# A two-layer trunk on one core: mask order in the DeltaNet layer, and wide products for most output blocks and the value blocks of three batches

## The chip, the cores and the metric

The kernel runs on one core of a Trainium2 chip. The metric is the device time of one execution in microseconds (us); lower is better. The kernel before takes 2536.62 us (median of three runs, 2536.11 to 2537.5).

## The reference

Input x has 256 tokens of 2048 channels, in float32. Two layers follow each other. Layer 0 is differential attention and a gated feed-forward block with a short causal convolution; layer 1 is a gated DeltaNet and a second feed-forward block. Each of the four parts is normalised ahead and added to x behind. The change lies in the DeltaNet, whose reference is, cut:

```python
def gated_deltanet(h, w_in, conv_w, a_log, dt_bias, norm_g, w_out):
    proj = h @ w_in
    qkv, z, b_gate, a_gate = jnp.split(proj, [...], axis=-1)
    qkv = jax.nn.silu(causal_dwconv(qkv, conv_w))
    q, k, v = jnp.split(qkv, [GDN_KEY_DIM, 2 * GDN_KEY_DIM], axis=-1)
    q = l2_norm(q...); k = l2_norm(k...)
    ...
    o = gated_delta_rule(q, k, v, g, beta)
    o = rms_norm(o, norm_g) * jax.nn.silu(z...)
    return o.reshape(...) @ w_out
```

There are 16 heads of queries and keys and 32 of values, each 128 wide. Inside the delta rule a decay `exp(g_i - g_j)` is taken where i >= j and zero elsewhere, and for every chunk of 64 tokens a triangular system is solved.

## The kernel before, in words

Activations lie transposed in SBUF: channels on the 128 partitions, tokens along the free axis. For precision every float32 operand is split into a rounded part and the rest: a weight tile becomes `whi` (ScalarE, line 89) and `wlo` (VectorE, line 90), and an activation has its two parts side by side. A product of a weight tile with an activation tile is three terms: high by high, low by high, high by low.

`dense` (line 132) makes one block: 128 or 256 output channels for 256 tokens, over 16 input tiles (8 in an output block of the DeltaNet), loaded four at a time from HBM into one of four slots. It has two forms. Wide: one product of 512 columns takes `whi` against both parts of the activation, and writes the two results beside each other in PSUM, and one of 256 columns takes `wlo` against the first part (lines 151 and 152). Narrow: three products of 256 columns, all added in the same 256 columns of PSUM (lines 151, 152 and 154). A pair of PSUM tiles (`ps`, two buffers) takes blocks by turns.

How a block leaves PSUM depends on the form. `merge` (line 177) multiplies a narrow block by the norm factor in one VectorE operation (line 196). A wide block has its second half copied by ScalarE (line 199), added by VectorE (line 200) and scaled by VectorE (line 205). `add_x` (line 340) adds a narrow block to x with one VectorE operation and a wide one with two (line 343). The feed-forward blocks are wide; in the DeltaNet all `dense` blocks are narrow.

The DeltaNet (`gdn`, line 542) does its 16 heads in four batches of four. The plan of a batch is: four blocks of queries and keys (k), the first block of values (v), two gate blocks (z, by `dense_tok`), and the other three blocks of values. Then come the eight output blocks of the batch before; those of the last batch follow at the end. Behind the blocks, generators go on one step at each `tick`, which `dense` calls after every load of four tiles: `keys` (per head: normalisation, decay, products of keys), `invert` (per batch: a triangular inversion in steps on VectorE, lines 654 and 657, with transposes in lines 661 and 663), `levels` (small products that finish the inverse, lines 691 to 725), `to_tokens` and `group` (the outputs of a pair of heads, lines 739 to 803, which leave the tiles `oc` for the output blocks).

What sets the order is this order of writing together with a planner, which simulates the time of every instruction when the kernel is built and so lays out each engine's list. On the chip each engine works off its list in order.

In `keys` a head squares its queries and keys (line 589), splits the squares in two parts (lines 321 and 322, tile `qp`, one buffer), fetches its decay rows from HBM by a broadcast DMA (line 594, tile `lt`), which can only begin once the gates' rows have been written there (line 902), adds the mask to them (line 610), sums the squares over the partitions on TensorE (`total`, line 329), takes an inverse root and the exponentials on ScalarE (lines 613 to 616) and scales (line 617). Two steps later the products of keys follow (lines 624 and 625).

Of the kernel before, what the change touches and what calls it, by code (L numbers as in the profile page):

```python
# [8 lines left out]
F32 = mybir.dt.float32  # L9
F32R = mybir.dt.float32r  # L10
AF = mybir.ActivationFunctionType
ALU = mybir.AluOpType
# [7 lines left out]
KD = D // P  # L20
# [6 lines left out]
class Trunk:  # L27
# [37 lines left out]
    def mp(self):  # L65
        return self.mps.tile([P, 512], F32, tag="mp", name="mp")
# [252 lines left out]
    def split(self, out, a):  # L319

        self.nc.scalar.copy(out[:, 0], a)
        self.nc.vector.tensor_tensor(out[:, 1], a, out[:, 0].bitcast(F32), ALU.subtract)

    def total(self, out, parts):

# [216 lines left out]
    def gdn(self, w_gate, w_in, w_z, w_out, nb, hb, gate_ap, const_ap, conv_col, ng, done):  # L542
# [7 lines left out]
        nc, tc, mp = self.nc, self.tc, self.mp  # L550
        nq = nb * hb
# [3 lines left out]
        with tc.tile_pool(name="gd", bufs=1) as gd:  # L555
# [13 lines left out]
                nc.gpsimd.memset(Tas[i][:64], 0.0)  # L569
            quad = [slice(32 * s, 32 * s + 32) for s in range(4)]  # L570
            flat = "p i c -> p (i c)"
            gates = {}

            def lin(ps):
                u = gd.tile([P, 2, T], F32, tag="u", name="u", bufs=1)
                self.merge(ps, u)
                return u

            def convs(u, tiles):
                c = gd.tile([P, 2, T], F32, tag="cv", name="cv", bufs=4)  # L580
                for i in range(2):
                    self.conv(c[:, i, :], u[:, i, :], [conv_col(t, tiles[i]) for t in range(4)], None)
                nc.scalar.activation(c, c, AF.Silu)
                return c

            def keys(hq, c, cc, b0, res):

                sq = gd.tile([P, 2, T], F32, tag="qs", name="qs", bufs=2)
                nc.scalar.square(sq, c)
                sp = gd.tile([P, 2, 2, T], F32R, tag="qp", name="qp", bufs=1)  # L590
                self.split(sp, sq)
                def fetch():
                    d = gd.tile([P, 2, 384], F32, tag="lt", name="lt", bufs=hb)
                    nc.sync.dma_start(d, gates["rows"][2 * hq:2 * hq + 2, :].unsqueeze(0).to_broadcast([P, 2, 384]))
                    return d

                d = fetch() if "rows" in gates else None
                yield
                yield
                while "rows" not in gates:  # L600
                    yield
                if d is None:
                    d = fetch()
                    yield
                    yield
                    yield
                gc = gates["col"]
                dv = d[:, :, :T].rearrange("p v (t c) -> p v t c", t=2)
                m4 = mask.unsqueeze(1).unsqueeze(1).to_broadcast([P, 2, 2, P])
                nc.vector.tensor_tensor(dv, dv, m4, ALU.add)  # L610
                pn = mp()
                with self.lnexp(self.total(pn, [sp])):
                    self.rsqrt(sq, self.apart(pn), 1)
                    for v in range(2):
                        for t, s in ((1, d[:, v, :P]), (0, d[:, v, P:])):
                            nc.scalar.activation(s, s, AF.Exp, bias=gc[:, t, 2 * hq + v:2 * hq + v + 1])
                nc.vector.tensor_tensor(c, c, sq, ALU.mult)
                q, k = c[:, 0, :], c[:, 1, :]
                yield
                yield  # L620
                prods = []
                for r in (k, q):
                    p = mp()
                    nc.tensor.matmul(p[:, :P], k[:, P:], r[:, P:], start=True, stop=True)
                    nc.tensor.matmul(p[:, P:384], k[:, :P], r, start=True, stop=True)  # L625
                    prods.append(p)
                lt = d
                qkt = gd.tile([P, 2, 384], F32, tag="qkt", name="qkt", bufs=hb)
                for v in range(2):
                    nc.vector.scalar_tensor_tensor(  # L630
                        qkt[:, v], prods[1][:, :384], P ** -0.5, d[:, v], ALU.mult, ALU.mult)
                    nc.vector.tensor_tensor(lt[:, v], prods[0][:, :384], d[:, v], ALU.mult)
                for v in range(2):
                    b = b0 + v
                    lv = lt[:, v, :T].rearrange("p (t c) -> p t c", t=2)
                    for r in quad:
                        nc.gpsimd.tensor_copy(
                            cc[r, :, 2 * b:2 * b + 2].rearrange("p c t -> p t c"), lv[r, :, r])
                    res.append((lt[:, v], qkt[:, v]))
# [89 lines left out]
            def to_tokens(c, vt, g, ready):  # L729
                yield  # L730
                yield
                p = mp()
                for t in range(2):
                    for i in range(2):
                        nc.tensor.transpose(p[:, (2 * t + i) * P:(2 * t + i + 1) * P], c[:, i, t * P:(t + 1) * P], ident)  # L735
                nc.scalar.copy(vt[:, :, g:g + 2, :], p.rearrange("p (t v c) -> p t v c", t=2, v=2))
                ready.append(g)
# [66 lines left out]

            def out(b, acts):
                for blk in range(KD // 2):
                    ps = self.dense(w_out[b * (KD // 2) + blk], 2 * hb, lambda k: self.await_(acts, k), wide=False)
                    self.add_out(blk, ps, done if b == nb - 1 else None, False)

            pg = self.dense(w_gate, KD, self.h_acts, tiles=1, wide=False)  # L810
            self.spawn(self.gates(gd, pg, nv, gp, ident, early, gates))
# [1 line left out]
            for b in range(nb):  # L813
                heads = range(b * hb, (b + 1) * hb)
                cc = gd.tile([P, 32, 32], F32, tag="s4", name="Cc", bufs=3)
                nc.gpsimd.memset(cc, 0.0)
                lqs, inv, solved, acts, zts = [], [], [], [], {}
                groups = [range(i, i + gh) for i in range(0, hb, gh)]
                plan = [("k", i) for i in range(hb)] + [("v", 0)] + [("z", g) for g in range(len(groups))]
                for op, i in plan + [("v", i) for i in range(1, hb)]:  # L820
                    if op == "k":
                        hq = heads[i]
                        c = convs(lin(self.dense(w_in[hq * 2], KD, self.h_acts, wide=False)), (hq, nq + hq))
                        self.spawn(keys(hq, c, cc, 2 * i, lqs))
                        if i == hb - 1:
                            self.spawn(invert(cc, lqs, inv))
                            self.spawn(levels(lqs, inv, range(len(groups)), solved))
                    elif op == "z":
                        gr = groups[i]
                        zt = zts[i] = gd.tile([P, 2, gv, P], F32, tag="vz", name="zt", bufs=4)  # L830
                        ps = self.dense_tok(w_z[heads[gr[0]] // 2], KD, self.h_acts)
                        for t in range(2):
                            nc.scalar.activation(zt[:, t].rearrange(flat), ps[:, t, :], AF.Silu,
                                                 scale=self.rstdc[:, t:t + 1])
                    else:
                        gi = i // gh
                        gr = groups[gi]
                        if i == gr[0]:
                            vt = gd.tile([P, 2, gv, P], F32, tag="vz", name="vt", bufs=4)
                            ready = []  # L840
                            self.spawn(group(gi, gr, lqs, solved, vt, ready, zts, acts))
                        hq = heads[i]
                        c = convs(lin(self.dense(w_in[hq * 2 + 1], KD, self.h_acts, wide=False)),
                                  (2 * nq + 2 * hq, 2 * nq + 2 * hq + 1))
                        self.spawn(to_tokens(c, vt, 2 * (i - gr[0]), ready))
                if pend:
                    out(*pend)
                pend = (b, acts)
            out(*pend)

    def gates(self, gd, pg, nv, gp, ident, early, res):
# [210 lines left out]
```

## Time and profile before

| | |
|---|---|
| Median of three runs | 2536.62 us |
| The profiled execution, whole | 2537.79 us |
| Its span, first to last instruction | 2536.1 us |
| The DeltaNet, from its first gate product to the last output product | 1054.5 to 1855.5 us |
| Granted TensorE clock | 1.000 |

In the rows that follow, PE is TensorE's products and PEld its weight loads, DVE is VectorE, ACT is ScalarE, SPq is the queue that issues the weights' DMAs. Lines such as L151 are lines of the kernel. A row of the timeline gives start, duration, engine, line, operation, output and inputs, and in brackets the idle time of that engine ahead of it with what released it. A group's row gives count, total busy time, mean duration in ns, and idle time before.

### The profile page before, as it was taken

To read this page: it belongs to the slowest core of one execution; us is meant where nothing else is said; L and a number is where in the kernel's file an instruction comes from. 1 tells how busy PE (TensorE), PEld (TensorE's weight loads), DVE (VectorE), ACT (ScalarE), POOL (GpSimd) and SP (SyncE) were. 2 spreads that over 40 slices of the span, in tenths; PEclk is the share of its full clock that TensorE was granted. 3 is DMA by queue.
4 is the path that set the end of the run, shared out by engine and by line. 5 is a ranking of instruction groups with operands and counts; after the bars stand their busy time and mean duration, and the time that the engine had idled before them with its cause. 6 is when DMAs were issued, how large, how long until landed. Compare 5 with 4: busy or idle time off the path is not lost.

```text
span 2536.1 us, 44059 instructions
## 1 busy us (share of the span) xinstructions
PE 2527.5 (100%) x17431; PEld 2354.5 (93%) x17431; DVE 1898.8 (75%) x2790; ACT 1505.4 (59%) x2076; POOL 91.6 (4%) x189
## 2 busy tenths in 40 slices
PE   9999999999999999999999999999999999999999
PEld 8998899999999999999999999999999999999998
DVE  8886677777777555679878788788787777776544
ACT  7766656666666444485674674674566666665443
POOL 0000000000000000010111011021000000000000
PEclk9999999999999999999999999999999999999999
DMA  7555566666666666666555565555466666666665
GB/s 254 176 183 174 167 205 201 201 201 201 201 202 202 198 203 201 201 192 199 161 174 184 167 185 179 171 182 178 159 200 201 202 200 202 201 201 207 208 208 157
DMA packets 138207, 487.34 MB, mean 192 GB/s; under 512 B 15472, under 2 KB 18448, under 8 KB 138000
## 3 DMA queue, kind: packets, MB, share of 16 engines
q1 hardware_dynamic: 137712, 484.17, 60.5%
q8 instruction: 137, 2.24, 0.4%
q14 instruction: 70, 0.57, 0.1%
q10 hardware_dynamic: 288, 0.35, 0.1%
HBM read 482.32 MB, written 2.15 MB: 191 GB/s over the span
## 4 chain that ended last, share of the span: by engine, by line
PE 99%; DMA 1%; DVE 0%; ACT 0%; SPq 0%; issue 0%
PE ps L151 47%; PE ps L152 27%; PE ps L154 7%; PE ps L220 3%; PE ps L221 3%; PE ps L222 3%; PE mp L752 2%; PE mp L151 1%; PE mp L329 1%; PE mp L625 1%; PE mp L152 0%; PE ps L123 0%; PE mp L717 0%; PE mp L735 0%; DMA raw<-w_first 0%; PE mp L797 0%
## 5 line engine op out<-in xcount | busy, mean ns | idle before, releaser
L90 DVE TENSOR_TENSOR wlo<-raw,whi 128x1024 fp32r<-128x1024 f32 (+2 forms) x911 | 1102.9, 1212 | 513.7 <-ACT whi L89 505.6
L89 ACT CAST whi<-raw 128x1024 fp32r<-128x1024 f32 (+2 forms) x911 | 944.4, 1038 | 864.7 <-PE ps L151 554.8
L151 PE MATMUL ps<-h,whi 128*128 128x512 f32 (+1 forms) x4208 | 1327.0, 356 | 0.0
L152 PE MATMUL ps<-h,wlo 128*128 128x256 f32 x4208 | 1151.0, 274 | 0.0
L151 PEld LDWEIGHTS ps<-h,whi 128*128 128x128 f32 x4208 | 798.3, 190 | 83.6
L152 PEld LDWEIGHTS ps<-h,wlo 128*128 128x128 f32 x4208 | 807.7, 192 | 0.9
L151 PE MATMUL ps<-ac,whi 128*128 128x512 f32 x1546 | 506.8, 382 | 0.0
L152 PE MATMUL ps<-ac,wlo 128*128 128x256 f32 x1546 | 421.2, 273 | 0.0
L151 PEld LDWEIGHTS ps<-ac,whi 128*128 128x128 f32 x1546 | 292.1, 189 | 40.8 <-PE ps L151 0.2
L152 PEld LDWEIGHTS ps<-ac,wlo 128*128 128x128 f32 x1546 | 296.8, 192 | 0.1
L154 PE MATMUL ps<-h,whi 128*128 128x256 f32 x1040 | 287.1, 276 | 0.0
L154 PEld LDWEIGHTS ps<-h,whi 128*128 128x128 f32 x1040 | 199.5, 192 | 0.4
L220 PE MATMUL ps<-whi,h 128*128 128x512 f32 x384 | 146.5, 382 | 0.0
L221 PE MATMUL ps<-wlo,h 128*128 128x512 f32 x384 | 146.0, 380 | 0.0
L222 PE MATMUL ps<-whi,h 128*128 128x512 f32 x384 | 145.9, 380 | 0.0
L310 DVE SCALAR_TENSOR_TENSOR cv<-u,fcols,cv 128x255 f32<-128x255 f32 (+1 forms) x344 | 142.7, 476 | 0.0
L151 PE MATMUL ps<-oc,whi 128*128 128x256 f32 x512 | 142.3, 278 | 0.0
L154 PE MATMUL ps<-oc,whi 128*128 128x256 f32 x512 | 141.9, 277 | 0.0
L152 PE MATMUL ps<-oc,wlo 128*128 128x256 f32 x512 | 141.5, 277 | 0.0
L154 PEld LDWEIGHTS ps<-oc,whi 128*128 128x128 f32 x512 | 98.2, 192 | 0.3
L152 PEld LDWEIGHTS ps<-oc,wlo 128*128 128x128 f32 x512 | 98.3, 192 | 0.2
L151 PEld LDWEIGHTS ps<-oc,whi 128*128 128x128 f32 x512 | 98.3, 192 | 0.1
(220 smaller groups left out, 2240.8 us busy)
## 6 DMA issues: line engine op xcount, KB each, us to landing
raw<-w_up SPq DMA_DIRECT2D x344, 512.0 KB, 4.8
raw<-w_down SPq DMA_DIRECT2D x160, 512.0 KB, 4.1
raw<-w_in SPq DMA_DIRECT2D x128, 512.0 KB, 4.6
raw<-w_z SPq DMA_DIRECT2D x64, 512.0 KB, 3.8
raw<-w_out SPq DMA_DIRECT2D x64, 512.0 KB, 4.3
raw<-w_qk SPq DMA_DIRECT2D x56, 512.0 KB, 4.6
raw<-w_v SPq DMA_DIRECT2D x32, 512.0 KB, 3.6
raw<-w_o SPq DMA_DIRECT2D x32, 512.0 KB, 4.5
```

The costliest lines, as they stand in the source:

```text
L89: self.cast = nc.scalar.copy(hi[:, :, s], raw[:, :, s])
L90: nc.vector.tensor_tensor(lo[:, :, s], raw[:, :, s], hi[:, :, s].bitcast(F32), ALU.subtract)
L151: nc.tensor.matmul(bank[c][:, :n], hi[:, k, s], self.turns(a[:, :n // T, :]), start=first, stop=False)
L152: nc.tensor.matmul(bank[c][:, :T], lo[:, k, s], self.turns(a[:, :1, :]), start=False, stop=last and wide)
L154: nc.tensor.matmul(bank[c][:, :T], hi[:, k, s], self.turns(a[:, 1:, :]), start=False, stop=last)
L220: nc.tensor.matmul(ps[:, c, :], ah, wh, start=first, stop=False)
L221: nc.tensor.matmul(ps[:, c, :], ah, wl, start=False, stop=False)
L222: nc.tensor.matmul(ps[:, c, :], al, wh, start=False, stop=last)
L310: nc.vector.scalar_tensor_tensor(out[:, j:], u[:, :T - j], taps[n - 1 - j], out[:, j:], ALU.mult, ALU.add)
L329: last = self.nc.tensor.matmul(out, self.onesr, self.pairs(p[:, j]), start=i + j == 0, stop=i + j == n)
L625: nc.tensor.matmul(p[:, P:384], k[:, :P], r, start=True, stop=True)
L752: nc.tensor.matmul(p[:, v, :], l(v), r[:, v, :], start=i == 0, stop=i == len(terms) - 1)
```

## The change

Three things are edited.

- Mask order. `split` returns its VectorE instruction, and `keys` keeps these in a list. The sum over partitions is written ahead of the mask addition. A head then goes on only when the first two heads have split their squares, and the mask addition is queued on VectorE behind a split: head 0's behind that of head 1, any other head's behind its own. Only head 0 waits for longer by this than before.
- Output blocks. All eight blocks of the last batch, and the last four of each of the other three batches, are wide.
- Value blocks. All four of each of the first three batches are wide. `lin` now calls `dense` itself, and for a wide block copies the second half into `u`, adds the first and scales, without a further tile.

```diff
     def split(self, out, a):
         self.nc.scalar.copy(out[:, 0], a)
-        self.nc.vector.tensor_tensor(out[:, 1], a, out[:, 0].bitcast(F32), ALU.subtract)
+        return self.nc.vector.tensor_tensor(out[:, 1], a, out[:, 0].bitcast(F32), ALU.subtract)
...
-            gates = {}
+            gates, lows = {}, []
-            def lin(ps):
+            def lin(w, wide):
+                ps = self.dense(w, KD, self.h_acts, wide=wide)
                 u = gd.tile([P, 2, T], F32, tag="u", name="u", bufs=1)
-                self.merge(ps, u)
+                if wide:
+                    main, small = self.halves(ps)
+                    uv = u.rearrange("p c (q j) -> p c q j", q=2)
+                    nc.scalar.copy(uv, small)
+                    nc.vector.tensor_tensor(uv, main, uv, ALU.add)
+                    self.scale(u)
+                else:
+                    self.merge(ps, u)
                 return u
...
-                self.split(sp, sq)
+                lows.append(self.split(sp, sq))
...
-                nc.vector.tensor_tensor(dv, dv, m4, ALU.add)
                 pn = mp()
-                with self.lnexp(self.total(pn, [sp])):
+                sums = self.total(pn, [sp])
+                while len(lows) < 2:
+                    yield
+                with tc.issue_after(lows[max(hq, 1)].ins):
+                    nc.vector.tensor_tensor(dv, dv, m4, ALU.add)
+                with self.lnexp(sums):
                     self.rsqrt(sq, self.apart(pn), 1)
...
                 for blk in range(KD // 2):
-                    ps = self.dense(..., wide=False)
-                    self.add_out(blk, ps, done if b == nb - 1 else None, False)
+                    wide = b == nb - 1 or blk >= KD // 4
+                    ps = self.dense(..., wide=wide)
+                    self.add_out(blk, ps, done if b == nb - 1 else None, wide)
...
-                        c = convs(lin(self.dense(w_in[hq * 2], KD, self.h_acts, wide=False)), (hq, nq + hq))
+                        c = convs(lin(w_in[hq * 2], False), (hq, nq + hq))
...
-                        c = convs(lin(self.dense(w_in[hq * 2 + 1], KD, self.h_acts, wide=False)),
+                        c = convs(lin(w_in[hq * 2 + 1], b<nb-1),
```

More of the change, by code (lines that the diff above doesn't have):

```diff
@@ L806, in out @@
                 for blk in range(KD // 2):
-                    ps = self.dense(w_out[b * (KD // 2) + blk], 2 * hb, lambda k: self.await_(acts, k), wide=False)
-                    self.add_out(blk, ps, done if b == nb - 1 else None, False)
+                    wide = b == nb - 1 or blk >= KD // 4
+                    ps = self.dense(w_out[b * (KD // 2) + blk], 2 * hb, lambda k: self.await_(acts, k), wide=wide)
+                    self.add_out(blk, ps, done if b == nb - 1 else None, wide)
             pg = self.dense(w_gate, KD, self.h_acts, tiles=1, wide=False)
```

## The prediction

> **What bounds the kernel now.** I read the page first, then the groups by form, then TensorE's rows in order of time in one wide and one narrow stretch, and last the rows around the one wait of TensorE in the stage that changes.
>
> ```profile
> span 2536.1 us, 44059 instructions
> PE 2527.5 (100%) x17431; PEld 2354.5 (93%) x17431; DVE 1898.8 (75%) x2790; ACT 1505.4 (59%) x2076; POOL 91.6 (4%) x189
> PE 99%; DMA 1%; DVE 0%; ACT 0%; SPq 0%; issue 0%
> ```
>
> Busy time, and the chain that ended last, say the same: the time is TensorE's list of products, from end to end. An edit pays only if it shortens that list, or takes out a place where TensorE stands still. The mean duration of a product is no price, since products overlap; the price is the distance from start to start. Two forms matter: wide (one product of 512 columns, one of 256) and narrow (three of 256). Here are the first and the last rows of a wide stretch and of a narrow one, 24 steps apart each.
>
> ```profile
> 700.12 0.38 PE L151 MATMUL ps<-h,whi 128*128 128x512 f32 x1
> 707.98 0.38 PE L151 MATMUL ps<-h,whi 128*128 128x512 f32 x1
> ...
> 1085.29 0.28 PE L151 MATMUL ps<-h,whi 128*128 128x256 f32 x1
> 1093.33 0.28 PE L151 MATMUL ps<-h,whi 128*128 128x256 f32 x1
> ```
>
> A wide pair takes (707.98 - 700.12) / 24 = 0.3275 us, a narrow triple (1093.33 - 1085.29) / 24 = 0.3350 us. Both stream 768 columns; the triple costs 7.5 ns more for one more product with its weight load.
>
> **Wide blocks: what TensorE saves.** The narrow third product (line 154) stands in these groups:
>
> ```profile
> L154 PE MATMUL ps<-h,whi 128*128 128x256 f32 x1040 | 287.1, 276 | 0.0
> L154 PE MATMUL ps<-oc,whi 128*128 128x256 f32 x512 | 141.9, 277 | 0.0
> ```
>
> A value block is 16 input tiles times 2 output tiles, 32 triples; three batches of four become wide: 12 x 32 = 384. An output block is 8 x 2 = 16 triples; 4 of 8 in three batches and all 8 in the last become wide: 20 x 16 = 320. So 704 triples become pairs: 704 x 7.5 ns = 5.3 us off the list. The two stretches read to 0.01 us each, 0.4 ns a step or 0.3 us in the sum; I take **5.2 us**, bounds 4.9 and 5.6.
>
> A page would price this lower, and it speaks against the change. The Trainium skill, "TensorE: Matmul & The Clock Gate", section "Back-to-back issue gap", gives the isolated gap of a warm product of N columns as N/2.4 + 2.5 ns, so an estimate by it is 3 x 109.2 - (215.8 + 109.2) = 2.5 ns a step, and 704 x 2.5 ns = 1.8 us in place of 5.2. The page itself says that this form misses the weight loads; the two stretches above differ by three times as much.
>
> **Wide blocks: what the other engines pay.** A narrow value block leaves PSUM in one VectorE operation (line 196). A wide one takes a ScalarE copy, a VectorE addition and a VectorE scaling, which the feed-forward stage already does at these prices:
>
> ```profile
> L199 ACT COPY mt<-ps 128x512 f32<-128x512 f32 x101 | 58.3, 577 | 0.0
> L200 DVE TENSOR_TENSOR u<-ps,mt 128x512 f32<-128x512 f32 x86 | 58.8, 684 | 0.0
> L205 DVE TENSOR_TENSOR u<-u,rstd 128x512 f32<-128x512 f32 x86 | 59.5, 692 | 3.0
> L196 DVE TENSOR_TENSOR u<-ps,rstd 128x512 f32<-128x512 f32 x32 | 22.0, 687 | 2.3 <-PE ps L154 1.7
> L343 DVE TENSOR_TENSOR x<-ps,x 128x512 f32<-128x512 f32 x78 | 53.7, 689 | 17.3 <-PE ps L154 12.1 <-PE ps L152 4.2
> ```
>
> So each of 12 value blocks adds 0.58 us to ScalarE and 0.684 + 0.692 - 0.687 = 0.69 us to VectorE; each of 20 output blocks adds a second addition to x, 0.69 us. No DMA, no weight cast and no table load goes or comes with this. The cover is thin only where VectorE is full, which is the stretch of the last three value blocks, where it also works off the inversion (lines 654 and 657). The next rows are those stretches of batches 0, 1 and 2, and behind the first the stretch that follows it.
>
> ```profile
> core 0: us, PE busy (x) PEld busy (x) DVE busy (x) ACT busy (x) POOL busy (x), PEclk, DMA share, GB/s
> 1166.90:1199.00 32.10, 32.10 (x290) 32.10 (x289) 30.99 (x59) 16.65 (x20) 0.00 (x0) 1.00 0.65 203
> 1199.00:1263.00 64.00, 64.00 (x737) 62.96 (x737) 52.62 (x86) 41.59 (x64) 7.94 (x13) 1.00 0.52 167
> 1321.70:1353.90 32.20, 32.20 (x291) 32.20 (x290) 31.38 (x59) 16.75 (x20) 0.00 (x0) 1.00 0.64 207
> 1519.40:1551.50 32.10, 32.10 (x290) 32.10 (x289) 30.56 (x62) 16.63 (x20) 0.00 (x0) 1.00 0.63 204
> ```
>
> VectorE has 1.1, 0.8 and 1.5 us free there and is asked for 3 x 0.69 = 2.1 us more: 0.6 to 1.3 us of inversion slides into the next stretch, where 64.0 - 52.6 = 11.4 us are free. TensorE's products wait for the weights, not for the inversion, in this stretch; I cost it at nothing, and if weights came late instead, at the sum of the three overruns, 1.0 + 1.3 + 0.6 = 2.9 us.
>
> The weights themselves are thin at one kind of place: the first gate block (z) behind the first value block. I counted casts and products in order, and found the least lead in batches 0 and 1; the cast's second half, and the first product that reads it:
>
> ```profile
> 1124.86 1.23 DVE L90 TENSOR_TENSOR wlo<-raw,whi 128x1024 fp32r<-128x1024 f32 x1 [2.04 <-ACT whi L89]
> 1127.25 0.38 PE L221 MATMUL ps<-wlo,h 128*128 128x512 f32 x1
> ...
> 1279.14 0.68 DVE L196 TENSOR_TENSOR u<-ps,rstd 128x512 f32<-128x512 f32 x1
> 1279.74 1.22 DVE L90 TENSOR_TENSOR wlo<-raw,whi 128x1024 fp32r<-128x1024 f32 x1
> 1281.62 0.38 PE L221 MATMUL ps<-wlo,h 128*128 128x512 f32 x1
> ```
>
> The leads are 1127.25 - 1126.09 = 1.16 us and 1281.62 - 1280.96 = 0.66 us. In batch 0 VectorE idles 2.04 us before the cast, so only the ScalarE copy (0.58) counts: 1.16 - 0.58 leaves 0.58. In batch 1 the merge stands right before the cast: 0.66 - 0.69 is just gone, and 0.58 more is missing if the copy also delays the cast. I take a new wait of **0.3 us**, bounds 0 and 0.7. PSUM has two such tiles; the second addition (0.69 us) falls in the 5.24 us of the block between and costs nothing while VectorE is less than that behind.
>
> In the last output blocks ScalarE and VectorE also make the next layer's input. There a block's VectorE work is two casts, two additions to x, two roundings and two sums of squares, and the period 16 x 0.3275 = 5.24 us:
>
> ```profile
> L90 DVE TENSOR_TENSOR wlo<-raw,whi 128x1024 fp32r<-128x1024 f32 x886 | 1082.1, 1223 | 488.8 <-ACT whi L89 480.8
> L235 DVE SCALAR_TENSOR_TENSOR h<-x,cols,h 128x256 fp32r<-128x256 f32 x48 | 21.1, 478 | 0.6 <-ACT h L234 0.6
> L247 DVE TENSOR_TENSOR ss<-ss,sq 128x256 f32<-128x256 f32 x45 | 18.9, 420 | 2.7 <-ACT whi L89 0.9
> ```
>
> 2 x (1.223 + 0.689 + 0.478 + 0.420) = 5.62 us is over it by durations; but neighbours overlap by some 0.08 us each (the rows at 1279.14 and 1279.74 start 0.60 apart at 0.68 long), so eight give 5.0. It fits, by little. A shortfall of 0.4 us a block, less what the weight slots hold ahead, is hidden; I cost it at nothing.
>
> **Mask order: what it saves.** Head 0's mask addition (line 610) waits for the transfer of the decay rows, and head 1's rounding (line 322), which TensorE needs, stands behind it on VectorE. From the chain and the engines' rows:
>
> ```profile
> 1098.77 6.36 DMA lt<-grow
> 1105.15 0.69 DVE lt L610
> ...
> 1104.66 0.28 PE L151 MATMUL ps<-h,whi 128*128 128x256 f32 x1
> 1106.50 0.48 PE L329 MATMUL mp<-qp,onesr 128*128 128x512 f32 x1 [1.56 <-DVE qp L322]
> ...
> 1115.01 0.72 DVE L617 TENSOR_TENSOR cv<-cv,qs 128x512 f32<-128x512 f32 x1
> 1116.64 0.39 PE L624 MATMUL mp<-cv 128*128 128x128 f32 x2
> ```
>
> TensorE starts 1106.50 - 1104.66 = 1.84 us apart where 0.11 is usual: 1.7 us stand still. With the mask queued behind head 1's rounding, this wait goes. What is late next is head 1's scaling (line 617): it ends at 1115.73 on a ScalarE chain that still starts at the landing, and line 624 would come 1.7 us sooner, at 1114.9, so 0.8 us comes back there. I take **0.9 us**, bounds 0 and 1.7. Behind the moved mask stand, on VectorE, the casts, and on ScalarE head 0's exponentials, which read the mask; both waited for that landing before. SP's and POOL's lists are not touched: the fetch is issued where it was.
>
> **Sum.** 5.2 + 0.9 - 0.3 = 5.8 us less. The profiled execution lasted 2537.79 us (span 2536.1), 1.17 above the median of the runs, 2536.62; it becomes 2532.0, span 2530.3, and the median 2536.62 - 5.8 = **2530.8 us**. A measurement of this kernel can tell about 0.2%, 5.1 us, from no change, so the line lies at 2531.5, and this forecast is just past it.
>
> **Rivals.** (1) Only the pitch is gained, and waits eat of it: the mask's stall merely moves (0 in place of 0.9), the z blocks cost their 0.7, and the three overruns come up in part. 5.2 - 0.7 = 4.5 with none of the overruns, 4.5 - 2.9 = 1.6 with all; the middle, 3.0, gives 2533.6. For it speaks how thin those leads are; against it that the other leads in these rows are several us.
> (2) The third weight load is hidden in these blocks, so that a step is worth its 768 columns in either form and saves nothing: 0.9 - 0.3 = 0.6, 2536.0. The two stretches speak against it, 24 steps each with nothing between. By the formula quoted from the Trainium skill it would lie between this and the forecast.
> (3) The other side: VectorE comes late for products that TensorE's fixed list places right behind its results. The end of batch 0's inversion and the product that reads it, and the one place where such a product is seen waiting:
>
> ```profile
> 1208.86 2.10 DVE L663 STREAM_TRANSPOSE tcc<-Ti 128x1024 f32<-128x1024 f32 x1
> 1211.65 0.54 PE L691 MATMUL mp<-tcc,lt 32*32 32x32 f32 x22
> ...
> 1565.92 1.11 PE L720 MATMUL mp<-Ta,lt 64*64 64x64 f32 x16 [0.23 <-DVE Ta L707]
> ```
>
> The margin is 1211.65 - 1210.96 = 0.7 us. If the list keeps its places, 4 x 0.69 = 2.8 us of added VectorE work make TensorE wait 2.1 us in each of three batches, 6.3; and each of the 12 added additions between the steps that follow can cost 0.5 more, 6: 12.3 - 6.1 gives 2542.8. It decides against the change from half of that on, 6.1 us. Against it: the list is planned anew with the added work in it, and before, nearly no product waits.
>
> **Chances.** Forecast 0.58 (own range 2529.0 to 2531.5); rival 1 0.25; rival 2 0.05; rival 3 0.12, of which 0.08 end slower by over 0.2% and 0.04 within. So faster 0.58, same 0.34, slower 0.08. Low end: the mask's full 1.7 and the pitch's 5.6 give 2529.3, less some slack for a list with fewer interruptions: 2528.8. High end, rival 1 with all of its waits: 2536.62 - 1.6 = 2535.0.
>
> **What would show it.** Right: line 154 at 656 products on h and 192 on oc, the pairs that replace them 0.3275 us apart, some 5 us less from the first gate product to the last output product; no 1.8 us gap at head 1's sum, and a smaller one at line 624. VectorE some 22 us busier (32 x 0.69), ScalarE 7 (12 x 0.58). Wrong: idle of TensorE released by the casts at the z blocks of batches 0 and 1, or by VectorE at lines 691 to 752 in batches 0 to 2; or the wide pairs not at the pitch of the feed-forward stage.

## The result, and the profile after

The changed kernel takes 2532.11 us (median of 18 runs, 2531.12 to 2532.9); the kernel before, in the runs beside it, 2536.6 (18 runs, 2535.72 to 2537.5). The ratio is 0.9982, with an interval of 0.9976 to 0.9989. So the change gains 4.5 us, 0.18%. That is clear of the noise and just short of the 0.2% (5.1 us) that the prediction had set as its line; the line lies inside the interval. The 2532.11 us lie between the prediction's ends (2528.8 to 2535.0), but outside the narrower range that it gave the forecast alone (2529.0 to 2531.5). Of all runs told of here, two of the kernel before and one of a later kernel had a granted TensorE clock of 0.95 or less; they are left out of the medians.

First, three lines of the page of the kernel after: the span, the busy time of each engine with its share and count, and the shares of the chain that ended last.

```profile
span 2529.5 us, 42709 instructions
...
PE 2522.4 (100%) x16727; PEld 2330.5 (92%) x16727; DVE 1913.4 (76%) x2822; ACT 1501.8 (59%) x2082; POOL 97.2 (4%) x189
...
PE 99%; DMA 1%; DVE 0%; ACT 0%; SPq 0%; issue 0%; ACTq 0%
```

TensorE still bounds the whole. It has 17431 - 16727 = 704 products fewer, and as many weight loads fewer. Which products these are stands in the groups by form (count, busy us, mean ns; then idle time before and what ended it):

```profile
L154 PE MATMUL ps<-h,whi 128*128 128x256 f32 x656 | 181.8, 277 | 0.0
L154 PE MATMUL ps<-oc,whi 128*128 128x256 f32 x192 | 53.1, 276 | 0.0
...
L580 ACT COPY u<-ps 128x512 f32<-128x512 f32 x12 | 6.9, 576 | 0.0
L581 DVE TENSOR_TENSOR u<-ps,u 128x512 f32<-128x512 f32 x12 | 8.2, 682 | 0.0
```

The third product of a step is gone 384 times on `h` and 320 times on `oc`; in their place stand twelve copies and twelve additions for the value blocks, and in `add_x` twenty more additions. The distance of two wide steps, 24 apart in a value block of batch 0, from TensorE's rows of the kernel after:

```profile
1175.83 0.38 PE L151 MATMUL ps<-h,whi 128*128 128x512 f32 x1
1183.69 0.38 PE L151 MATMUL ps<-h,whi 128*128 128x512 f32 x1
```

(1183.69 - 1175.83) / 24 = 0.3275 us, the pitch of the feed-forward stage. Next is the length of the DeltaNet. The first product of it and the first product of the next stage, before and then after:

```profile
1054.47 0.28 PE L151 MATMUL ps<-h,whi 128*128 128x256 f32 x1
1855.45 0.38 PE L151 MATMUL ps<-h,whi 128*128 128x512 f32 x1
```

```profile
1053.94 0.28 PE L151 MATMUL ps<-h,whi 128*128 128x256 f32 x1
1848.87 0.38 PE L151 MATMUL ps<-h,whi 128*128 128x512 f32 x1
```

That is 800.98 and 794.93 us, 6.05 less. The stages behind it keep their length to 0.1 us, and what lies ahead is 0.53 us shorter in this execution. Below, "the stage" is always this length, read from the same two products of each trace. A second profile of each kernel gave 800.90 and 794.84, within 0.1 us of the first, where medians of the same kernel differ by 0.3 to 0.4 us.

TensorE's one larger wait of the stage, from its rows of the kernel after (in brackets the idle time and what released it):

```profile
1112.27 0.38 PE L151 MATMUL ps<-h,whi 128*128 128x512 f32 x1
1113.22 0.38 PE L152 MATMUL ps<-h,wlo 128*128 128x256 f32 x1 [0.57 <-DVE wlo L90]
```

The two start 0.95 us apart where 0.22 is usual: 0.73 us stand still, in the first value block of batch 0, for the second half of a weight cast. The 1.7 us stall at head 1's sum is gone. What VectorE and ScalarE do ahead of it, from their rows in order of time:

```profile
1101.22 0.69 DVE L322 TENSOR_TENSOR qp<-qs,qp 128x512 fp32r<-128x512 f32 x1
1103.84 0.69 DVE L624 TENSOR_TENSOR lt<-lt,con 128x512 f32<-128x512 f32 x1 [1.93 <-DMA lt<-grow]
...
1110.70 0.69 DVE L322 TENSOR_TENSOR qp<-qs,qp 128x512 fp32r<-128x512 f32 x1 [1.49 <-ACT qp L321]
1111.31 0.72 DVE L624 TENSOR_TENSOR lt<-lt,con 128x512 f32<-128x512 f32 x1
1111.96 1.21 DVE L90 TENSOR_TENSOR wlo<-raw,whi 128x1024 fp32r<-128x1024 f32 x1
```

```profile
1103.99 1.28 ACT L629 ACT_TABLE_LOAD   x1
1105.28 1.50 ACT L629 ACTIVATE lt<-lt,gc 128x128 f32<-128x128 f32 x4
1106.80 1.28 ACT L297 ACT_TABLE_LOAD   x1
1108.09 0.69 ACT L316 ACTIVATE qs<-mp,eps 128x512 f32<-128x512 f32 x1
1108.68 1.48 ACT L629 ACTIVATE lt<-lt,gc 128x128 f32<-128x128 f32 x4
1110.06 0.60 ACT L321 CAST qp<-qs 128x512 fp32r<-128x512 f32 x1
1110.57 1.05 ACT L89 CAST whi<-raw 128x1024 fp32r<-128x1024 f32 x1
```

Head 1's rounding (line 322, at 1101.22) now stands ahead of the first mask addition (now line 624), so TensorE's sum no longer waits for the landing. Behind it ScalarE is busy without a gap: two table loads (`ACT_TABLE_LOAD`), the exponentials of two heads, an inverse root, then a head's cast and at last the weight's `whi`, done at 1111.62. VectorE takes the weight's second half at 1111.96, 0.34 us later, behind one more mask addition (1111.31).

The three late value blocks of batches 0, 1 and 2, the same stretches as before, by windows (stretch, length, then busy time and count of each engine):

```profile
core 0: us, PE busy (x) PEld busy (x) DVE busy (x) ACT busy (x) POOL busy (x), PEclk, DMA share, GB/s
1165.00:1196.60 31.60, 31.60 (x195) 29.08 (x194) 30.95 (x59) 17.73 (x23) 0.00 (x0) 1.00 0.62 201
1319.00:1350.40 31.40, 31.40 (x194) 28.86 (x194) 30.09 (x59) 17.35 (x22) 0.37 (x2) 1.00 0.57 186
1515.20:1546.60 31.40, 31.40 (x193) 28.85 (x192) 30.95 (x58) 17.54 (x22) 0.00 (x0) 1.00 0.63 205
```

TensorE is busy from end to end and the clock is whole; VectorE is as full as it was, and PEld falls from all of the time to 92% of it.

### The profile page after: what moved, and what is told of

Read it like the earlier page. It is cut to its first block, busy times and chain, and to the rows that moved or that the text cites. A ratio compares the mean times of both kernels' runs of the same rounds, so it can differ in the third digit from the quotient of the medians.

```text
span 2529.5 us, 42709 instructions
## 1 busy us (share of the span) xinstructions
PE 2522.4 (100%) x16727; PEld 2330.5 (92%) x16727; DVE 1913.4 (76%) x2822; ACT 1501.8 (59%) x2082; POOL 97.2 (4%) x189
## 4 chain that ended last, share of the span: by engine, by line
PE 99%; DMA 1%; DVE 0%; ACT 0%; SPq 0%; issue 0%; ACTq 0%
PE ps L151 50%; PE ps L152 27%; PE ps L154 4%; PE ps L221 3%; PE ps L220 3%; PE ps L222 3%; PE mp L765 2%; PE mp L151 1%; PE mp L329 1%; PE mp L638 1%; PE mp L152 0%; PE ps L123 0%; PE mp L730 0%; PE mp L748 0%; PE mp L810 0%; PE mp L466 0%
## 5 line engine op out<-in xcount | busy, mean ns | idle before, releaser
L151 PE MATMUL ps<-h,whi 128*128 128x512 f32 (+1 forms) x4208 | 1348.0, 366 | 0.0
L151 PEld LDWEIGHTS ps<-h,whi 128*128 128x128 f32 x4208 | 797.2, 189 | 93.6 <-ACT zt L847 0.2
L154 PE MATMUL ps<-h,whi 128*128 128x256 f32 x656 | 181.8, 277 | 0.0
L151 PE MATMUL ps<-oc,whi 128*128 128x512 f32 (+1 forms) x512 | 159.7, 344 | 0.0
L154 PEld LDWEIGHTS ps<-h,whi 128*128 128x128 f32 x656 | 125.8, 192 | 0.2
L151 PEld LDWEIGHTS ps<-oc,whi 128*128 128x128 f32 x512 | 97.4, 190 | 8.0
L308 ACT ACTIVATE cv<-u,fcols 128x256 f32<-128x256 f32 x172 | 93.9, 593 | 0.6 <-DVE u L205 0.5
L310 DVE SCALAR_TENSOR_TENSOR cv<-u,cols,cv 128x255 f32<-128x255 f32 (+2 forms) x192 | 84.2, 478 | 0.4 <-ACT cv L306 0.3
```

What stands on the lines that cost most here:

```text
L151: nc.tensor.matmul(bank[c][:, :n], hi[:, k, s], self.turns(a[:, :n // T, :]), start=first, stop=False)
L154: nc.tensor.matmul(bank[c][:, :T], hi[:, k, s], self.turns(a[:, 1:, :]), start=False, stop=last)
L308: nc.scalar.activation(out, u, AF.Identity, bias=bias, scale=taps[n - 1])
L310: nc.vector.scalar_tensor_tensor(out[:, j:], u[:, :T - j], taps[n - 1 - j], out[:, j:], ALU.mult, ALU.add)
```

## The experiments

The theory: the stage gets shorter by the list (704 x 7.5 ns) and by the mask's stall less what comes back. The rivals: waits eat the gain (1), the third weight load was hidden anyway (2), VectorE comes late (3). What had to be told apart is the worth of each part alone, why the mask's wait comes back where it does, and whether VectorE's margin is near its end.

| | median, us | ratio to before (interval) | stage, us | against before |
|---|---|---|---|---|
| before, two profiles | 2536.6 to 2537.0 | | 800.98, 800.90 | |
| mask order alone | 2537.46 | 1.0004 (0.9995 to 1.0013) | 800.69 | -0.29 |
| output blocks alone | 2534.32 | 0.9990 (0.9981 to 0.9999) | 798.51 | -2.47 |
| value blocks alone | 2535.29 | 0.9995 (0.9986 to 1.0004) | 799.30 | -1.68 |
| both blocks, old mask order | 2532.75 | 0.9984 (0.9975 to 0.9993) | 796.51 | -4.47 |
| the change, run again | 2531.83 | 0.9980 (0.9971 to 0.9989) | 794.84 | -6.14 |

"Against before" is against the first profile's 800.98. Each part alone moves the median by 2.6 us or less, where an interval reaches 2.3 us to either side, so the stage has to speak.

### The parts alone

Mask order alone. The diff is against the change:

```diff
-                    wide = b == nb - 1 or blk >= KD // 4
+                    wide = False
...
-                        c = convs(lin(w_in[hq * 2 + 1], b<nb-1),
+                        c = convs(lin(w_in[hq * 2 + 1], False),
```

> Mask order alone, all blocks narrow. Theory A (the parts add up; the mask order exchanges a stall of 1.7 us for a shorter wait on the same landing): 0.9 to 1.0 us under the kernel before, about 2535.6, no gap of 1.8 us ahead of head 1's sum, and a wait of 0.3 to 0.8 us some 10 us later. Rival B (most of what the whole change gained in its median, 4.5 us, is not the list, and the profile of before is a slow execution whose stall is longer than usual): 0.0 to 0.4 us under, no difference that can be told.

The stall at head 1's sum went, as it should, and a wait for the same weight cast as in the change came, here in a narrow block:

```profile
1113.37 0.38 PE L152 MATMUL ps<-h,wlo 128*128 128x256 f32 x1 [0.80 <-DVE wlo L90]
```

The stretch from the first gate product to the end of the first value block gained 0.76 us, but one gap of 0.56 us appeared later among the small products of the inverse (at 1385.5), whose row names no releaser, and the stage was only 0.29 shorter. The median shows no gain.

Output blocks alone:

```diff
-                sums = self.total(pn, [sp])
-                while len(lows) < 2:
-                    yield
-                with tc.issue_after(lows[max(hq, 1)].ins):
-                    nc.vector.tensor_tensor(dv, dv, m4, ALU.add)
-                with self.lnexp(sums):
+                nc.vector.tensor_tensor(dv, dv, m4, ALU.add)
+                with self.lnexp(self.total(pn, [sp])):
...
-                        c = convs(lin(w_in[hq * 2 + 1], b<nb-1),
+                        c = convs(lin(w_in[hq * 2 + 1], False),
```

> Wide output blocks alone, 20 of 32. Theory A: 320 steps x 7.5 ns = 2.4 us under the kernel before, about 2534.2; the eight output blocks of the last batch 42.75 - 128 x 0.0075 = 41.8 us long, and no product waiting for VectorE. Rival C (the second additions make VectorE late for the small products between them): less than 1.5 us under, with waits at lines 691 to 752 of the old numbering.

320 steps x 7.5 ns are 2.4 us; the stage lost 2.47. This is the term of the list with nothing beside it, and no wait on VectorE came. The mask's stall stood where it was:

```profile
1106.24 0.48 PE L329 MATMUL mp<-qp,onesr 128*128 128x512 f32 x1 [1.52 <-DVE qp L322]
```

Value blocks alone: the old mask order as above, and

```diff
-                    wide = b == nb - 1 or blk >= KD // 4
+                    wide = False
```

> Wide value blocks of three batches alone. Theory A: 384 steps x 7.5 ns = 2.9 us, less up to 0.7 us at the z blocks: 2.2 to 2.9 under, about 2534.0; three value blocks in a row 0.7 us shorter in batches 0 to 2 and unchanged in batch 3. Rival D (the merge of a wide value block holds up the weight casts): idle of TensorE released by the casts behind value blocks, 1.5 us under or less.

384 steps are worth 2.9 us, and the stage lost 1.68. Two waits took more than the difference: the stretch of the gate blocks of batch 1 got 0.89 longer, and a gap of 0.64 with no releaser stood at 1385.2, as with the mask alone. The stall at head 1's sum gave 0.6 back: it was shorter here (0.94 us of idle).

Both kinds of block, with the old mask order as above:

> Both wide parts, old mask order. Theory A: 5.2 us under the kernel before, about 2531.4, less up to 0.7 at the z blocks; the stall at head 1's sum is there as before. That would be below the whole change's 2532.1 only if the new mask order costs. Rivals C and D: 3 to 4 us under, 2533, with the loss shown as idle of TensorE released by VectorE or ScalarE.

The list is worth 5.3, and the stage lost 4.47. Again the gate stretch of batch 1 is 0.89 longer, and here is a wait in it, for a head's scaled keys:

```profile
1274.55 0.38 PE L222 MATMUL ps<-whi,h 128*128 128x512 f32 x1
1275.28 0.38 PE L633 MATMUL mp<-cv 128*128 128x128 f32 x1 [0.35 <-DVE cv L626]
```

In the change this stretch has its old length (47.55 us after, 47.56 before). So the mask order is worth 0.29 us alone, and 796.51 - 794.93 = 1.58 us on top of the wide blocks. None of the 1.58 lies where the mask's stall was: from the first gate product to the end of the first value block this kernel with the old mask order takes 66.07 us, the change 66.15. The change is shorter by 0.43 in the gate stretch of batch 0, by 0.89 in that of batch 1 and by 0.51 between the two; elsewhere it gives 0.25 back in all. The parts don't add: each edit makes the planner lay out the lists anew, and waits of 0.3 to 0.9 us come and go between these kernels, far from the edited lines.

The old stall itself differed between these kernels, which all have the old mask order: 1.52 us of idle with the outputs, 0.94 with the values, 0.49 with both. It goes with the two transfers that the first mask addition waits for, the write of the gates' rows and the fetch behind it. From the chain of the kernel with both wide blocks, in order of time (start, duration):

```profile
1095.33 3.67 DMA grow<-early
1099.01 4.52 DMA lt<-grow
```

These are 8.2 us; the two took 9.2 us with the outputs, 8.6 with the values, and 9.3 in the kernel before, whose fetch of 6.36 us stands in the prediction. Why the transfers differ isn't shown.

The change run once more, unchanged:

> The changed kernel once more, unchanged, for a second profile. Theory A (the DeltaNet stage is shorter by the 5.2 us of the list and by what the mask order gains, and what differs between profile and median is the length of the start and of the wait on the decay rows): DeltaNet stage 794.9 us within 0.5, median again 4 to 5 us under the kernel before. Rival E (the profile of the changed kernel was a lucky one in the DeltaNet stage): 796 us or more.

Both the gain and the stage came back, 0.9980 and 794.84.

### What the wait at the first value block hangs on

The theory for the wait that came back was first the landing of the decay rows, since the exponentials follow on it; the other was ScalarE's own list. To take the landing away, the rows were fetched from a constant input, so that the decay and its bias are left out:

```diff
-                    nc.sync.dma_start(d, gates["rows"][2 * hq:2 * hq + 2, :].unsqueeze(0).to_broadcast([P, 2, 384]))
+                    nc.sync.dma_start(d, const_ap[2 * hq:2 * hq + 2, :].unsqueeze(0).to_broadcast([P, 2, 384]))
...
-                            nc.scalar.activation(s, s, AF.Exp, bias=gc[:, t, 2 * hq + v:2 * hq + v + 1])
+                            nc.scalar.activation(s, s, AF.Exp)
```

> The changed kernel, but the decay rows are fetched from a constant input, so that the fetch does not wait for the gates' rows to be written (the exponentials have no bias, and the decay is left out). Theory A (the wait of 0.6 to 0.7 us on a weight cast in batch 0 comes from the landing of these rows): it is gone or under 0.2 us, the DeltaNet stage 0.5 to 0.9 us shorter, 2531.4. Rival (it comes from ScalarE's table loads alone): the wait stays.

It took 2535.76 us, ratio 0.9995 (0.9986 to 1.0004). The wait at 1113 was gone, but a greater one came at the gates:

```profile
1073.82 0.38 PE L878 MATMUL mp<-con,glin 64*128 64x64 f32 x2 [2.71 <-DVE glin L196]
```

Freed of its wait, the fetch of the first rows was issued at 1055.98, ahead of most of the first weights; ScalarE's first casts then waited 1.6 and 1.8 us for the weights, and TensorE for them. The same edit in the kernel before:

> The kernel before with the same edit (decay rows from a constant input, decay left out). Theory A: the stall of 1.7 us at head 1's sum is gone, 1 to 1.7 us under the kernel before, 2535.3; then the mask order has nothing left to save, and the stretch from the first gate product to the end of the first value block is as long as that of the changed kernel with the same edit plus 0.24 us for the wide value block. Rival (the stall is the order on VectorE, whatever the landing): it stays at over 1 us.

It took 2543.06 us, ratio 1.0025 (1.0015 to 1.0034): the stall at head 1's sum went, and one of 3.26 us came at the same gate product. Behind both waits the granted clock was 0.50 for some 3 us. So neither run prices the landing; both price a fetch that goes ahead of weights. A second profile of the kernel before, for the spread of its stage:

> The kernel before, unchanged, for a second profile. Theory A: start of 28.2 to 28.9 us, DeltaNet stage 800.0 to 801.0 us, the stall at head 1's sum between 0.6 and 1.7 us, as the two kernels with the old mask order had it. Rival E (the first profile is typical in all): stall 1.7 and stage 801.0 again.

It gave 2537.46 us, a stage of 800.90, and the stall at head 1's sum again, with 1.61 us of idle against 1.56: rival E holds. Then the same edit in the change, with each fetch queued behind the latest load of weights:

```diff
-                    nc.sync.dma_start(d, gates["rows"][2 * hq:2 * hq + 2, :].unsqueeze(0).to_broadcast([P, 2, 384]))
+                    with tc.issue_after(self.loaded.ins):
+                        nc.sync.dma_start(d, const_ap[2 * hq:2 * hq + 2, :].unsqueeze(0).to_broadcast([P, 2, 384]))
...
-                            nc.scalar.activation(s, s, AF.Exp, bias=gc[:, t, 2 * hq + v:2 * hq + v + 1])
+                            nc.scalar.activation(s, s, AF.Exp)
```

> The changed kernel with the decay rows fetched from a constant input (decay left out), and each fetch queued behind the latest weight load, so that it does not run ahead of the weights as it did in the first form of this test. Theory A (the wait of 0.57 to 0.73 us on a weight cast in the first value block comes from the late landing of these rows): the wait is gone, no wait at the gates, stage 794.9 - 0.7 = 794.2 us or somewhat less. Rival (ScalarE's table loads and casts alone): a wait of 0.4 us or more stays there.

It took 2530.71 us (2530.31 to 2531.43), ratio 0.9975 (0.9966 to 0.9985), with no wait at the gates. TensorE's wait was still there, and ScalarE still had no gap ahead of it:

```profile
1112.91 0.38 PE L152 MATMUL ps<-h,wlo 128*128 128x256 f32 x1 [0.30 <-DVE wlo L90]
```

```profile
1105.72 1.13 ACT L630 ACTIVATE lt<-lt 128x128 f32<-128x128 f32 x4
...
1108.74 1.11 ACT L630 ACTIVATE lt<-lt 128x128 f32<-128x128 f32 x4
...
1110.26 1.05 ACT L89 CAST whi<-raw 128x1024 fp32r<-128x1024 f32 x1
```

The products start 0.67 us apart here, 0.45 over the usual, against 0.73 over it in the change. The two groups of exponentials are 0.37 us shorter each without their bias, and `whi` is done 0.31 us sooner; that alone covers the 0.28 us. So in the profiled execution the landing isn't what the wait hangs on. By the rows it hangs on ScalarE's list, exponentials, table loads and casts one behind the other with a weight's cast at their end, and for some 0.3 us on the mask addition that stands on VectorE ahead of the weight's second half. No run took either of these out.

### How far wide blocks carry

All blocks of 256 channels wide, the keys' too:

```diff
-                    wide = b == nb - 1 or blk >= KD // 4
+                    wide = True
...
-                        c = convs(lin(w_in[hq * 2], False), (hq, nq + hq))
+                        c = convs(lin(w_in[hq * 2], True), (hq, nq + hq))
...
-                        c = convs(lin(w_in[hq * 2 + 1], b<nb-1),
+                        c = convs(lin(w_in[hq * 2 + 1], True),
```

> Every block of 256 channels of the DeltaNet wide: the blocks of keys, the values of the last batch and the first four output blocks too. That is 512 + 128 + 192 = 832 steps more. Theory A: the list is 832 x 7.5 ns = 6.2 us shorter than the changed kernel's; each block of keys adds 0.58 us to ScalarE and 0.69 us to VectorE where the first batch has almost no lead left (0.05 us at the third load of its first value block), so 1 to 2 us come back as waits on the casts in batch 0: 4 to 5 us under the changed kernel, about 2527.5. Rival (the wide form pays only where VectorE is free): not faster than the changed kernel, with waits for the casts in all batches.

It took 2571.57 us, ratio 1.0133 (1.012 to 1.0147), with a stage of 836.8. TensorE waited 3.24 us until ScalarE had read a gate block out of PSUM (into `zt`), behind the second gate block of batch 1, and such waits came again. By windows, TensorE's busy time and the granted clock around that one, and around a wait of 5.13 us for the last inversion:

```profile
core 0: us, PE busy (x), PEclk, DMA share, GB/s
1320.00:1324.00 4.00, 0.76 (x6) 0.89 0.82 266
1324.00:1329.00 5.00, 5.00 (x16) 0.50 0.05 19
1329.00:1334.00 5.00, 5.00 (x30) 0.91 0.28 77
...
1804.00:1809.00 5.00, 0.48 (x4) 0.88 0.54 179
1809.00:1816.00 7.00, 6.33 (x171) 0.50 0.23 77
1816.00:1824.00 8.00, 6.24 (x60) 0.50 0.00 0
```

These waits cost more than their length: behind them the granted clock is 0.50, for some 5 us in the first place, with 16 products where the next 5 us have 30, and for 15 in the second. The Trainium skill, "TensorE: Matmul & The Clock Gate", section "Why this matters for your kernels", asks for no idle gaps of TensorE over about 3 us, since the clock falls back to a half behind them; the 3.24 us here agree.

The key blocks alone on top of the change (the middle edit above):

> The changed kernel with the blocks of queries and keys wide as well (16 blocks, 512 steps, 3.8 us off the list). All blocks wide lost 40 us against the changed kernel, with TensorE waiting behind the second gate block and at half clock for some us after each wait. Theory F (the merge of the blocks of keys, 0.58 us of ScalarE and 0.69 of VectorE each, delays the chain of a head's normalisation, and with it the inversion and all that hangs on it): this kernel shows the waits behind the gate blocks and a late inversion, 15 to 40 us slower than the changed kernel. Rival G (it was the values and output blocks of the ends that did it): within 4 us of the changed kernel.

It took 2543.34 us (nine runs), ratio 1.0023 (1.0013 to 1.0032), 11.2 over the change's 2532.1, between what theory F and rival G had named. It shows the same 3.24 us wait behind a gate block of batch 1, with the clock at 0.50 for 5 us behind it, waits of 0.7 to 0.8 us for casts in the gate blocks of batch 0, and a late chain at the end. The other engines were not full there: from 1269.0 to 1323.3, the gate blocks of batch 1 up to the end of the wait, VectorE was busy for 42.5 us of 54.3 and ScalarE for 42.4. What TensorE waited for is the end of a chain on ScalarE:

```profile
1320.11 0.58 ACT L749 COPY vt<-mp 128x512 f32<-128x512 f32 x1 [0.70 <-PE mp L748]
1320.70 1.28 ACT L847 ACT_TABLE_LOAD   x1
1321.99 2.42 ACT L847 ACTIVATE zt<-ps,rstd 128x512 f32<-128x512 f32 x4
```

The copy waits for small products that TensorE's list has behind the gate block's last one (1317.95), and the activations that free the block's PSUM tiles stand behind the copy. In the change the same copy and table load run from 1315.61 to 1317.49, ahead of the block's last product (1318.65). So it is the order of the lists that costs here; why the planner lays them out so with wide key blocks isn't shown.

The other half: all output blocks and the last batch's values wide, on top of the change (the first and the last edit above):

> The changed kernel with all output blocks and the values of the last batch wide, keys narrow: 192 + 128 = 320 steps more, 2.4 us off the list. Theory F: no wait behind the gate blocks; the last batch's inversion ends up to 2 us later, and 0 to 2 us come back behind it: 0.4 to 2.4 us under the changed kernel, about 2530.5. Rival G: 15 us slower or more, with TensorE waiting on the inversion of the last batch.

It took 2539.04 us, ratio 1.0011 (1.0002 to 1.002), 7 over the change where theory F expected a gain and rival G 15 us, with a stage of 802.57. Two of the waits, from TensorE's rows, and the stretch around the second, by windows:

```profile
1761.90 0.45 PE L151 MATMUL ps<-oc,whi 128*128 128x512 f32 x1 [1.56 <-DVE x L343]
1804.20 0.30 PE L810 MATMUL mp<-con,zt 128*128 128x128 f32 x1 [2.70 <-DVE zt L799]
```

```profile
core 0: us, PE busy (x), PEclk, DMA share, GB/s
1800.00:1804.00 4.00, 1.50 (x12) 1.00 0.15 57
1804.00:1808.00 4.00, 3.59 (x17) 0.57 0.41 131
1808.00:1812.00 4.00, 4.00 (x34) 1.00 0.00 0
```

The first is a PSUM tile that the second addition to x gave back late; the second is the chain of the last batch, behind which no next batch stands to cover it. This is rival 3's kind of wait, and here it decides. No version that computes the whole ran faster than the change itself.

## Why the prediction was right or wrong

**The list: right.** 5.2 us were predicted. The output blocks alone gave 2.47 for 2.4, the pitch in the value blocks is 0.3275 us, and rival 2 falls with it. An estimate by the Trainium skill's formula, "TensorE: Matmul & The Clock Gate", section "Back-to-back issue gap", which comes to 2.5 ns a step, is 320 x 2.5 ns = 0.8 us for the output blocks, a third of what they gave.

**The mask: the stall went, but not for the price of the prediction.** 0.9 us were predicted: 1.7 of stall, less 0.8 that come back. The stall at head 1's sum went. But what was late next wasn't line 624 of before, the products of keys: it was the weight cast of the first value block, with 0.73 us. The step followed head 1's scaling from the landing, and didn't follow what stands behind it on ScalarE. The stretch from the gates to the end of the first value block got 1.23 us shorter (67.38 to 66.15), of which 32 x 7.5 ns = 0.24 is the list: 1.0. That this lies so near 0.9 is luck. With both kinds of wide blocks and the old mask order the same stretch got 1.31 shorter, and with the mask order alone 0.76. Over the whole stage the mask order gave 0.29 alone and 1.58 on top of the wide blocks, and that 1.58 lies at the gate blocks and between them.

**The wait at the gate blocks: wrong.** 0.3 us were added; in the change the stretch of batch 1 is as long as before. With the old mask order it is there, and greater than its bound (0.89 against 0.7), though the wait seen in it is one for a head's scaled keys and not for a cast. The prediction priced wide blocks in the old order of the lists; the planner made a new one.

**The cover of VectorE: right.** The three late value blocks overran nothing: each such stretch fell by 0.7 us (32.15 to 31.49 and 31.44 in batches 0 to 2, for 96 x 7.5 ns), and in batch 3, whose blocks stayed narrow, it kept its 32.16. The small products did not keep their places, as rival 3 needs: in batch 1 the inversion's last transposition starts at 1386.92 instead of 1374.36, and the first product that reads it at 1390.56 instead of 1377.17, with no wait. The eight last output blocks went from 42.88 to 41.92 us, which is their 128 steps, 0.96 us. That the cover there is thin is right as well: four more wide blocks in each of the other batches and in the last one's values broke it.

**Busy times: wrong.** VectorE rose by 14.6 us, not 22: the durations of its operations rose by 21.1 (2042.0 to 2063.1, count times mean over all groups), but neighbours overlap, and an overlap counts once. ScalarE fell by 3.6 where 7 more were predicted. Most of this is table loads, at 1.283 us each, of which the prediction wrote for the wide blocks that none "goes or comes": before has 57, both kinds of wide blocks alone 54, the mask order alone 49, the change 51. The mask order adds and drops no operation of ScalarE, so the count goes with the order of its list.

**The sum.** The stage was to lose 5.8 us and lost 6.05, and the profiled execution was to take 2532.0 us and took 2531.32. Of the 6.05 some 5.3 are the list. The other 0.8 stand where the prediction had 0.9 - 0.3 = 0.6, but two errors met there, a mask order that gave its gain in another place and a gate wait that didn't come; that this much fits is luck.

The medians moved by 4.5 and 5.0 us in the two comparisons, where 5.8 was taken for them too. The step that failed is the last one, from the profile to the median: the prediction put the gain of one profiled execution on the median as it stood. The profiles of before lay 1.2 and 0.5 us above the medians of their kernel (2537.79, 2537.46), those of after 0.8 and 0.7 below (2531.32, 2531.16). So the result lies on the near side of the 0.2% line, which the forecast had passed by 0.7 us only.

A gain of 4.5 is also the figure of rival 1 without its overruns: the pitch less 0.7 at the gate blocks. Its waits are not in the two profiles of the change, where batch 1's gate stretch has its old length and the mask's stall came back at less than half. Whether they stand in other executions wasn't shown, and so what the typical execution pays that the profiled one doesn't stays open. One candidate is the landing of the decay rows: with it taken away, the median (2530.71) lay 1.1 to 1.4 us below the change's, and the runs spread 1.1 us instead of 1.8, though the stage was only 0.3 shorter. That is an argument from two numbers, and shorter exponentials are in it as well.

## What to carry to other kernels

Where TensorE's list is the bound, price a form of product by the distance from start to start in a stretch without waits: 7.5 ns a step predicted 2.4 of a measured 2.47 us. A wider form moves work to other engines, and pays only where the new lists bring no wait for that work; twenty output blocks and twelve value blocks took it here, the key blocks and the rest of the outputs and values didn't. With this planner an edit's waits couldn't be priced one by one: the parts gave 0.3, 2.5 and 1.7 us alone and 6.05 together.

## What the runs showed that was not expected

- The clock can fall behind waits shorter than the 3.24 us: behind the wait of 2.70 us above, the mean granted clock of the next 4 us is 0.57, which is a half for most of them. The Trainium skill's rule of about 3 us, named above, would have let this one pass. Length alone doesn't decide: a wait of 1.94 us with all blocks wide was also followed by 0.57 over 4 us, one of 2.27 us with the key blocks wide by 1.00.
- A DMA that is freed of its wait isn't free: with the fetch issued ahead of weights, TensorE waited 2.7 us at the gates in one kernel and 3.3 in the other.
- Gaps of 0.56 and 0.64 us for which no row names a releaser stood among the smallest products of the inverse with the mask order alone and with the value blocks alone, and in neither of the two kernels compared. They stay unexplained.
